# Cross-attention queries of a two-layer encoder by seven half-width products instead of eight

## The chip, the cores and the metric

The program runs on one core of one Trainium2 chip, in one launch. Its time is the device time in microseconds (us), the median of several executions. Beside the times there is one execution taken by the hardware profiler; all durations below come from it.

The engines are named as in the profile: PE is the matrix engine (PEld its weight loads), DVE the vector engine, ACT the scalar engine, POOL the general-purpose engine, SP the engine that only issues transfers.

## The reference, cut to what matters

The model has two layers over 512 positions of width 1024. Each layer is a mixer, a cross-attention to a memory of 256 rows, and a gated feed-forward block with a short convolution. The change touches the cross-attention, and what stands just ahead of it:

```python
x = x + mixed                                        # mixed = mixer's heads @ w_out
x = x + memory_cross_attention(rms_norm(x, xattn_norm[layer]), rms_norm(mem, mem_norm[layer]),
                               xattn_wq[layer], xattn_wkv[layer], xattn_wo[layer])

def memory_cross_attention(xn, memn, wq, wkv, wo):   # 4 heads of 256
    q = split_heads(xn @ wq, 4)                      # 512x1024 @ 1024x1024
    k, v = split(memn @ wkv, 2)
    logits = einsum('bhqd,bhmd->bhqm', q, k) * 256 ** -0.5
    p = softmax(logits, axis=-1)
    return merge_heads(einsum('bhqm,bhmd->bhqd', p, v)) @ wo
```

`rms_norm(x, gain)` is `x * rsqrt(mean(x*x) + eps) * gain`: one factor for each position (the inverse root) and one for each channel (the gain). All of it is float32.

## The kernel before, in words

**Numbers in two parts.** A float32 operand is split into a rounded part (`hi`, a copy by ACT) and the rest (`lo`, a subtraction by DVE). A product of two operands is then three matmuls (`mm3`, lines 291 to 293). A weight block is 128 x 1024: loaded by SP into `raw` (three buffers), copied by ACT into `wh` (L285), subtracted by DVE into `wl` (L282).

**Layout.** Channels lie on partitions: x is eight tiles `x[k]` of 128 channels x 512 positions, and `xh[k]`, `xl[k]` are the two parts of x times the gain, without the inverse root. A block of the projection is 8 channel blocks x 3 = 24 matmuls of 128 x 512, all into one PSUM bank.

**Mixer's output projection** (`p_out`). For each m of 8, 24 matmuls make output block m; DVE adds it into `x[m]` (`xadd`, L619), then `xprep` makes `xh[m]`, `xl[m]` (ACT L603, DVE L604) and adds the squares of x (ACT L597, DVE L598).

**Cross-attention** (`xattn`). `x_norm` sums the squares over channels by two matmuls (L497), takes the inverse root in eight steps of DVE and ACT, and leaves it spread over all partitions in `rb`. For each head h of 4: two key blocks (two heads' worth were already made during the mixer by `p_fill`), two query blocks of 24 matmuls each, whose evacuation multiplies by `rb` and splits (`query`: DVE L1177, ACT L285, DVE L282), the value blocks for every second head, four score tiles of 6 matmuls each with their softmax (maximum L1213, exponential L1214, reciprocal L1218), the transposes, and the weighted values. Then the output projection, again by `p_out`, which also makes four `forms` of x for the feed-forward block.

**The feed-forward block already uses seven products.** 21 of its 22 pairs of blocks are done by a scheme of Strassen and Winograd (`seven` in `ffn_steps`): a 2 x 2 block product by seven products of half size, with sums of weight quarters (`sa`, made by a load and a second load that POOL issues and that adds in memory, L1505; `sb`, by DVE) and sums of x quarters (`form_steps`, L1280 to L1296). Each of its products is 12 matmuls of 128 x 256.

**Order.** The kernel's own planner (`Plan`) takes items by priority as their inputs and buffers become ready and writes the instructions of all engines in one fixed order; each engine then runs its own list strictly in that order, waiting on semaphores. The feed-forward block has a second planner (`Sched`). Both orders are decided when the program is built.

Of the kernel before, what the change touches and what calls it, by code (L numbers as in the profile page):

```python
# [236 lines left out]
class Builder:  # L237
# [475 lines left out]
    def q_parts(self, ps):  # L713
        nc, mp = self.nc, self.mp
        tq = self.til(mp, "tmp")
        nc.vector.scalar_tensor_tensor(out=tq[:], in0=ps[:], scalar=-0.125, in1=self.rb, op0=ALU.mult, op1=ALU.mult)
        out = []
        for s in range(2):
            a, b = slice(64 * s, 64 * s + 64), slice(64 - 64 * s, 128 - 64 * s)
            qa = self.til(mp, f"qa{s}", dtype=F32R, bufs=2)  # L720
            nc.scalar.copy(qa[a, :], tq[a, :])
            self.sub(qa[b, :], tq[a, :], qa[a, :])
            out.append(qa)
        return out

    def k_parts(self, ps, par):
# [4 lines left out]
        for s in range(2):  # L731
            a, b = slice(64 * s, 64 * s + 64), slice(64 - 64 * s, 128 - 64 * s)
            ka = self.til(mp, f"ka{s}", dtype=F32R, bufs=2)
# [110 lines left out]
    def mix0(self):  # L844
        nc, t, tc = self.nc, self.t, self.tc
        with tc.tile_pool(name="mix0", bufs=1, reuse_waits="tile") as mp:
            self.mp = mp
# [9 lines left out]
            mh, ml = ([None if k in (2, 3) else mp.tile([P, SEQ], F32R, name=f"{n}{k}") for k in range(8)] for n in ("mh", "ml"))  # L857
# [123 lines left out]
            for p_ in range(4):  # L981
# [41 lines left out]
                def weigh(p_=p_, pts=[i[2] for i in items], v=v):  # L1023
# [10 lines left out]
                    if mh[p_] is None:  # L1034
                        mh[p_], ml[p_] = (self.til(mp, ("ka", "qa")[p_ - 2] + i, dtype=F32R) for i in "01")
# [11 lines left out]
            self.p_out(pl, t["wo0"], lambda: (mh, ml), kd, "xat", 0, [4, 5, 6, 7, 0, 1, 2, 3], 100, True, self.memnorm)  # L1047
            pl.run()
# [73 lines left out]

    def xattn(self, layer):
        nc, t, tc = self.nc, self.t, self.tc
        with tc.tile_pool(name=f"xa{layer}", bufs=1, reuse_waits="tile") as mp:
            self.mp = mp
            pl = Plan(self.plan, [st["banks"][0] for st in self.fills], s=2, w=2, e=4, q=2, pt=2, wt=3)
            for tag, n, bufs in (("sa", 1024, 3), ("ra", 512, 1)):
                self.til(self.kp, tag, (P, n), bufs=bufs)
            kv = [self.til(self.kp, f"kv{i}", (P, 1024), F32R, bufs=1) for i in range(8)]  # L1130
            self.pad(self.kp, 128)
            kth, ktl = ([v[:].rearrange("p (a b) -> p a b", b=MEM) for v in vs] for vs in (kv[:2], kv[2:4]))
            vh, vl = kv[4:6], kv[6:]
            for tag in ("tmp", "nh"):
                self.til(mp, tag, bufs=1 + (tag == "tmp"))
            self.pad(mp, 64)
            for tag in ("qh0", "ql0", "qh1", "ql1"):
                self.til(mp, tag, dtype=F32R)
            self.pad(mp, 192)
            for tag in ("pth", "ptl"):  # L1140
                self.til(mp, tag, (P, 2, 512), F32R)
            norm = self.x_norm(pl, (mp, "nh", 1), 0, deps=self.xdone[7])
            mh, ml = [None] * 8, [None] * 8
            kd = {}
            ve = []
            for h in range(4):
                p = 10 + 10 * h
                ke = []
                for m in (2 * h, 2 * h + 1):

                    def keys(ps, m=m, at=0):
                        tmp = self.til(mp, "tmp")
                        nc.vector.tensor_tensor(out=tmp[:, :MEM], in0=ps[:, at : at + MEM], in1=self.memrb, op=ALU.mult)
                        self.split(kth[m // 4][:, m % 4, :], ktl[m // 4][:, m % 4, :], tmp[:, :MEM])

                    kc = (("D", 0.34), ("A", 0.34), ("D", 0.34))
                    if m < 2 * len(self.fills):
# [3 lines left out]
                                lambda keys=keys, st=st, m=m: keys(st["ps"], at=m % 2 * MEM), 0, (), p, free=("acc",) if m % 2 else (), chain=kc, st=st,  # L1161
# [6 lines left out]
                            pl, t["xk"][layer, m], self.mems, keys, kc, prio=p, n=MEM, per=4, off=OFF  # L1168
                        )
                    )  # L1170
                qs = {}
                qe = []
                for d in range(2):

                    def query(ps, d=d, qs=qs):
                        tmp = self.til(mp, "tmp")
                        nc.vector.scalar_tensor_tensor(out=tmp[:], in0=ps[:], scalar=0.0625, in1=self.rb, op0=ALU.mult, op1=ALU.mult)  # L1177
                        qs[d] = (self.til(mp, f"qh{d}", dtype=F32R), self.til(mp, f"ql{d}", dtype=F32R))
                        self.split(qs[d][0][:], qs[d][1][:], tmp[:])

                    qe.append(
                        self.p_proj(
                            pl, t["xq"][layer, 2 * h + d], self.xs, query, (("D", 0.66), ("A", 0.52), ("D", 0.6)), kdeps=self.xdone, edeps=[norm], prio=p, eorder=list(qe),
                            etake=("q",) if d == 0 else (),
                        )
                    )
                if h % 2 == 0:
# [5 lines left out]
                    ve = self.p_proj_tok(pl, t["xv"][layer, h // 2], self.mems, 2, values, prio=p)  # L1193
                pts = {}

                def ptget(pts=pts):
                    pts["h"] = self.til(mp, "pth", (P, 2, 512), F32R)
                    pts["l"] = self.til(mp, "ptl", (P, 2, 512), F32R)

                got = pl.add(ptget, 0, qe, p + 5, take=("pt",))  # L1200
                ss, ts = [], []
                for i in range(4):
# [3 lines left out]
                    def score(h=h, qs=qs, res=res, sl=sl):  # L1206
                        sp = self.bank("s")
                        for d in range(2):
                            kb = 2 * h + d
                            self.mm3(sp[:, :MEM], qs[d][0][:, sl], qs[d][1][:, sl], kth[kb // 4][:, kb % 4, :], ktl[kb // 4][:, kb % 4, :], d == 0, d == 1)  # L1210
# [3 lines left out]
                        nc.scalar.activation(e[:], sp[:, :MEM], AF.Exp, bias=sm[:, 0:1], accum_out=sm[:, 1:2])  # L1214
# [12 lines left out]
                    a = pl.add(score, 3 * MM, ke + qe, p + 5, take=("s", "e"), free=("s",), chain=(("D", 0.35), ("A", 0.5)))  # L1227
# [5 lines left out]
                for d in range(2):  # L1233

                    def weigh(h=h, d=d, pts=pts):
# [5 lines left out]
                        mh[b], ml[b] = (self.til(mp, "mixed", dtype=F32R, bufs=8) if h < 2 else self.til(self.memp, "mem", dtype=F32R, bufs=8) for _ in range(2))  # L1241
                        self.split(mh[b][:], ml[b][:], ps[:])

                    ws.append(pl.add(weigh, 6 * MM, ts + ve, p + 5, take=("w",), free=("w",), chain=(("A", 0.5), ("D", 0.6))))
# [3 lines left out]
            self.forms = []  # L1248
            used = [d for k in kd for d in kd[k]]

            def form(k):
                th, tl = (self.til(self.kp, f"kv{i + k}", (P, 1024), F32R, bufs=1) for i in (0, 4))
# [3 lines left out]
                f, r = self.til(mp, "pth", (P, 2, 512)), self.til(mp, "ptl", (P, 1024))  # L1256
                for fn in self.form_steps(k, layer, f, r, th, tl):
                    fn[1]()

            for k in range(4):  # L1260
                pl.add(
                    lambda k=k: form(k), 0, [*used, *self.xdone[2 * k + 1]], 100 + 2 * k + 2, order=[last_form] if k else [],
                    chain=(("A", 1.5), ("D", 1.4), ("A", 1.0), ("D", 1.2)) if k < 3 else (),
                )
                last_form = pl.items[-1]
# [3 lines left out]
    def form_steps(self, k, layer, t, r, th, tl):  # L1269
# [6 lines left out]
            t[:, j, :], self.x[2 * k + j][:], AF.Identity, scale=self.col("ffn", layer * 8 + 2 * k + j)  # L1276
# [16 lines left out]
    def ffn_steps(self, layer, mp):  # L1293
# [22 lines left out]
        RAWS = {"raw": (self.wp, 1024, 3), "dr": (mp, 512, 2), "sa": (self.kp, 1024, 3), "sb": (mp, 512, 2), "ra": (self.kp, 512, 1)}  # L1316
# [81 lines left out]
        small_ = lambda tag: [self.til(mp, tag + i, dtype=F32R, bufs=1) for i in "hl"]  # L1398
        act_ = lambda: tuple(self.til(mp, i, dtype=F32R, bufs=10) for i in ("ah", "al"))
        self.pad(mp, 64)  # L1400
        for tag in ("s2", "a22", "s4"):
# [662 lines left out]
```

## Time and profile before

| what | value |
|---|---|
| median of 3 executions | 1464.67 us (1464.3 to 1464.98) |
| the profiled execution: its time, its span | 1464.19 us, 1462.4 us |
| PE busy | 1447.1 us, 99% of the span |
| weight loads (PEld) busy | 1272.8 us, 87% |
| DVE busy | 1219.0 us, 83% |
| ACT busy | 891.0 us, 61% |
| TensorE clock granted over the span | 0.999 |
| layer 0: mixer's output projection; queries, keys, values and attention; its output projection | about 217 to 262; 262 to 345; 345 to 408 us |
| layer 1: the same | about 923 to 968; 968 to 1051; 1051 to 1115 us |

A busy PE is a PE with matmuls in flight: they overlap, so a matmul's duration (0.39 us for 128 x 512) is longer than the step from its start to the next one's. The price of a matmul is that step. Instructions of DVE and ACT overlap their neighbours a little too, so there also the step from start to start counts where they stand in a row.

### The profile page before, as it was taken

The numbers are of one execution on the slowest core, as the hardware profiler recorded it, in microseconds if no ns is written. First come the engines' busy times: TensorE is split into PE (matmuls) and PEld (weight loads), VectorE is DVE, ScalarE is ACT, GpSimd is POOL, SyncE is SP. The second block draws the span as 40 slices with busy tenths as digits, with TensorE's granted clock in tenths as the row PEclk, the third lists the DMA queues.
The fourth block names the chain that finished last, engine by engine and source line by source line (L and its number), as shares of the span: only waits on it lengthen the run. The fifth ranks groups of instructions, "written<-read, shape, count | busy, mean of one in ns | idle before, by whom it ended". The sixth has DMA issues, their size and how long they took to land.

```text
span 1462.4 us, 23179 instructions
## 1 busy us (share of the span) xinstructions
PE 1447.1 (99%) x8719; PEld 1272.8 (87%) x8719; DVE 1219.0 (83%) x2172; ACT 891.0 (61%) x1581; POOL 67.9 (5%) x108
## 2 busy tenths in 40 slices
PE   9999999999999999999999999999999999999998
PEld 7888787888899999999888888888888999999987
DVE  7789985766799999999769988676569999999974
ACT  7688664544577666666447665455456766656654
POOL 0001120000000000000000100000000000000000
PEclk9999999999999999999999999999999999999999
DMA  5222433723246666662223332363323666665322
GB/s 199 87 74 73 122 117 123 209 87 116 87 133 164 170 170 159 155 163 75 84 101 109 115 102 68 128 175 121 115 83 112 157 182 168 158 164 153 110 69 76
DMA packets 67297, 183.91 MB, mean 126 GB/s; under 512 B 7264, under 2 KB 7264, under 8 KB 67184
## 3 DMA queue, kind: packets, MB, share of 16 engines
q1 hardware_dynamic: 60128, 159.28, 34.0%
q0 software_dynamic: 6048, 22.02, 8.7%
q8 instruction: 68, 1.11, 0.3%
q10 hardware_dynamic: 1008, 1.12, 0.2%
q14 instruction: 45, 0.37, 0.1%
HBM read 180.27 MB, written 2.13 MB: 125 GB/s over the span
## 4 chain that ended last, share of the span: by engine, by line
PE 82%; DVE 11%; ACT 3%; issue 2%; DMA 1%; POOL 0%; SPq 0%; DVEq 0%; ACTq 0%; POOLq 0%
PE acc L291 16%; PE acc L292 16%; PE acc L293 16%; PE w L292 5%; PE w L293 5%; PE w L291 5%; PE s L293 3%; PE s L291 3%; PE s L292 3%; DVE wl L282 2%; PE acc L352 2%; PE acc L354 2%; PE acc L353 2%; DVE c L1449 1%; PE w L800 1%
## 5 line engine op out<-in xcount | busy, mean ns | idle before, releaser
L291 PE MATMUL acc<-xh,wh 128*128 128x512 f32 (+1 forms) x752 | 258.0, 343 | 0.1
L293 PE MATMUL acc<-xh,wl 128*128 128x512 f32 (+1 forms) x752 | 255.9, 340 | 0.2 <-DVE wl L282 0.2
L292 PE MATMUL acc<-xl,wh 128*128 128x512 f32 (+1 forms) x752 | 255.6, 340 | 0.0
L282 DVE TENSOR_TENSOR wl<-raw,wh 128x1024 fp32r<-128x1024 f32 (+2 forms) x193 | 228.9, 1186 | 23.3 <-ACT wh L285 22.7
L285 ACT CAST wh<-raw 128x1024 fp32r<-128x1024 f32 (+1 forms) x135 | 139.2, 1035 | 139.1 <-PE acc L292 85.5
L293 PEld LDWEIGHTS acc<-xh,wl 128*128 128x128 f32 x752 | 141.2, 188 | 17.3 <-DVE wl L282 0.6
L291 PEld LDWEIGHTS acc<-xh,wh 128*128 128x128 f32 x752 | 141.4, 188 | 16.6 <-ACT v L1685 0.6
L292 PEld LDWEIGHTS acc<-xl,wh 128*128 128x128 f32 x752 | 141.3, 188 | 16.1
L1449 DVE SCALAR_TENSOR_TENSOR c<-hs,vec,c 128x512 f32<-128x512 f32 x176 | 128.0, 744 | 6.9 <-ACT c L1442 5.9
L293 PE MATMUL w<-ah,wl 128*128 128x512 f32 x304 | 119.0, 392 | 0.0
L292 PE MATMUL w<-al,wh 128*128 128x512 f32 x304 | 118.6, 390 | 0.0
L291 PE MATMUL w<-ah,wh 128*128 128x512 f32 x304 | 118.5, 390 | 0.0
L1442 ACT ACTIVATE c<-hs,vec 128x512 f32<-128x512 f32 x88 | 70.8, 815 | 35.9 <-DVE hs L1589 35.3
L293 PEld LDWEIGHTS w<-ah,wl 128*128 128x128 f32 x304 | 57.1, 188 | 12.1
L619 DVE TENSOR_TENSOR x<-w,x 128x512 f32<-128x512 f32 x72 | 49.4, 686 | 20.0 <-PE w L293 20.0
L291 PEld LDWEIGHTS w<-ah,wh 128*128 128x128 f32 x304 | 57.1, 188 | 9.9
L292 PEld LDWEIGHTS w<-al,wh 128*128 128x128 f32 x304 | 57.1, 188 | 9.9
L1505 POOL DMA_DIRECT2D sa<-in_up_dram x42 | 36.1, 860 | 610.2 <-DMA sa<-in_up_dram 162.1
L1520 ACT CAST wh<-sa 128x1024 fp32r<-128x1024 f32 x42 | 44.1, 1050 | 32.5 <-PE w L292 24.0
L291 PE MATMUL acc<-mem,wh 128*128 128x256 f32 (+1 forms) x192 | 61.1, 318 | 0.0
L292 PE MATMUL acc<-mem,wh 128*128 128x256 f32 (+1 forms) x192 | 60.9, 317 | 0.0
L293 PE MATMUL acc<-mem,wl 128*128 128x256 f32 (+1 forms) x192 | 60.7, 316 | 0.0
(475 smaller groups left out, 4190.9 us busy)
## 6 DMA issues: line engine op xcount, KB each, us to landing
raw<-in_up_dram SPq DMA_DIRECT2D x46, 512.0 KB, 3.5
sa<-in_up_dram SPq DMA_DIRECT2D x42, 512.0 KB, 3.9
sa<-in_up_dram POOLq DMA_DIRECT2D x42, 512.0 KB, 5.8
dr<-in_down_dram SPq DMA_DIRECT2D x64, 256.0 KB, 3.1
ra<-in_up_dram SPq DMA_DIRECT2D x42, 256.0 KB, 2.6
raw<-in_xk_dram SPq DMA_DIRECT2D x16, 512.0 KB, 4.3
raw<-in_wo_dram SPq DMA_DIRECT2D x16, 512.0 KB, 3.6
raw<-in_xq_dram SPq DMA_DIRECT2D x16, 512.0 KB, 3.3
```

What stands on the lines that cost most here:

```text
L282: self.nc.vector.tensor_tensor(out=lo, in0=v, in1=hi.bitcast(F32), op=ALU.subtract)
L285: self.nc.scalar.copy(hi, v)
L291: mm(out, wh, xh, start=first, stop=False, skip_group_check=parts)
L292: mm(out, wh, xl, start=False, stop=False, skip_group_check=parts)
L293: mm(out, wl, xh, start=False, stop=last, skip_group_check=parts)
L352: mm(ps, xh[k][:, ts], wh[:, ws], start=(k == 0), stop=False)
L353: mm(ps, xh[k][:, ts], wl[:, ws], start=False, stop=False)
L619: self.nc.vector.tensor_tensor(out=self.x[m][:], in0=ps[:], in1=self.x[m][:], op=ALU.add)
L1442: nc.scalar.activation(st["c_"][:, j, :], hs()[:, j, 2:514], AF.Identity, scale=self.col("cw", (layer * 3 + 2) * 44 + blk), bias=self.col( ...
L1449: nc.vector.scalar_tensor_tensor(out=c, in0=hs()[:, j, n : n + 512], scalar=w, in1=c, op0=ALU.mult, op1=ALU.add)
L1505: return add("POOL", 0.0029 * cols, lambda: nc.gpsimd.dma_start(out(), src(), accum_op=ALU.add), deps, due, (), (), 6.0)
L1520: nc.scalar.copy(s["wh"][:, :cols], raw())
```

## The change

The query projection of each head is computed by the feed-forward block's scheme: the head's two blocks of 128 query channels and the two halves of 256 positions make a 2 x 2 block product over the halves (even and odd blocks) of the input channels, done by seven products of 12 matmuls of 128 x 256.

- `p_forms`, called at the end of both mixers' plans, closes the mixer's tile pool, opens the pool that the cross-attention and the feed-forward block share, issues the first loads of weight sums, makes the forms of x for the block pairs 0 to 2 during the output projection, and issues the first product of heads 0 and 1.
- `p_query` is one head's seven products. Heads 0 and 1 are interleaved in finer pieces around the arrival of the last block of x (`x[7]`); heads 2 and 3 follow whole.
- The fourth form is made at the start of `xattn` (`last`).
- The evacuation no longer multiplies by the inverse root. `x_norm` goes; four matmuls of 128 x 2 (`rsqrt_cols`) and twelve DVE instructions of four columns make the inverse root for 128 positions per partition, and the exponential takes it as its scale. The maximum is multiplied by it first, one DVE instruction of one column for each score tile.
- Keys that were made during the mixer, all other keys, and the values are evacuated only after all four heads' products, because the forms lie in the tiles where keys and values will lie (`opened`, priority 45; heads now have priority 50 and up).
- Tiles that outlive the mixers move to pools of their own (`out0`, `out1`); several tiles of `xattn` and of the feed-forward block share buffers under new names.

```diff
+    def p_forms(self, pl, layer, mix, used):
+        def opened():
+            mix.close()
+            self.kp = self.keys.enter_context(self.tc.tile_pool(name=f"keys{layer}", bufs=1, side="right", reuse_waits="tile"))
...
+            for h in range(3):
+                self.sum_load(layer, h)
+        def form(k):
...
+            for fn in self.form_steps(k, "xat", layer, f[:, :1024].rearrange("p (a b) -> p a b", a=2), r[:, :1024], th, tl):
+                fn[1]()
+        last = pl.add(opened, 0, used, 100, order=[self.memnorm])
+        for k in range(3):
+            last = pl.add(
+                lambda k=k: form(k), 0, self.xdone[2 * k + 1], 100 + 2 * k + 2, order=[last], chain=(("A", 1.5), ("D", 1.4), ("A", 1.0), ("D", 1.2))
+            )
...
+    def sum_load(self, layer, h):
+        sa = self.sums[h] = self.til(self.kp, "sa", (P, 1024), bufs=3)
+        a1, a2 = self.t["xq"][layer, 2 * h], self.t["xq"][layer, 2 * h + 1]
+        pair = self.t["xq"][layer].rearrange("(h j) p c -> h p j c", j=2)[h]
+        self.nc.sync.dma_start(sa[:].rearrange("p (a b) -> p a b", a=2), pair[:, :, :512])
+        self.nc.gpsimd.dma_start(sa[:], a2, accum_op=ALU.add)
...
+    def p_query(self, pl, layer, h, order):
...
+        def product(w, c, xs, bank, first, ks=range(4)):
+            for k in ks:
+                at = slice(c + k * P, c + (k + 1) * P)
+                self.mm3(st[bank][:, :256], w[0][:, at], w[1][:, at], *xs(k), first and k == 0, k == 3, True)
...
+        def p1():
+            st["raw"] = self.til(self.wp, "raw", (P, 1024), bufs=3)
+            nc.sync.dma_start(st["raw"][:], a1)
...
+            st["f3"] = self.parts(OFF)
+            self.split(*st["f3"], st["raw"][:])
+            st["X"] = self.bank("w")
+            product(st["f3"], 0, X(0, 0), "X", True)
+        def seed():
+            st["Y"] = self.acc_bank(st["banks"][0])
+            nc.scalar.activation(st["Y"][:, :256], st["X"][:, :256], AF.Copy, scale=-1.0)
+        def p5():
+            st["f1"] = self.parts(OFF)
+            self.split(*st["f1"], self.sums[h][:])
+            st["R"] = self.bank("s")
+            product(st["f1"], 512, T1, "R", True, range(4 - (h == 0)))
+        def kept(n, bank):
+            st[n] = self.til(mp, "xe", (P, MEM), bufs=4)
+            nc.scalar.copy(st[n][:], st[bank][:, :256])
+        def p6():
+            st["sb"] = self.til(self.kp, "sb", bufs=2)
+            tt_(out=st["sb"][:], in0=self.sums[h][:, 512:], in1=st["raw"][:, :512], op=ALU.add)
...
+            wide("s2", st["sb"][:])
+            product(st["s2"], 0, T2, "Y", False, range(4 - (h == 0)))
+        def c11():
+            st["hs"] = self.til(mp, "hs", (P, 1088))
+            nc.scalar.copy(quarter(0, 0), st["X"][:, :256])
+        def p3():
+            tt_(out=st["sb"][:], in0=st["sb"][:], in1=st["raw"][:, 512:], op=ALU.add)
+            wide("s4", st["sb"][:])
+            product(st["s4"], 0, X(1, 1), "R", False)
+        def p4():
+            wide("a22", self.rest[:])
...
+            product(st["a22"], 0, T4, "Y", False)
...
-            norm = self.x_norm(pl, (mp, "nh", 1), 0, deps=self.xdone[7])
+            norm = pl.add(
+                lambda state=self.state: rs.append(self.rsqrt_cols(state["sq"], SEQ, 256.0 / DM, 256.0 * EPS)), 0.4, self.xdone[7], 2.5, take=("s",), free=("s",), chain=(("D", 2.3),)
+            )
...
-                    def query(ps, d=d, qs=qs):
-                        tmp = self.til(mp, "tmp")
-                        nc.vector.scalar_tensor_tensor(out=tmp[:], in0=ps[:], scalar=0.0625, in1=self.rb, op0=ALU.mult, op1=ALU.mult)
-                        qs[d] = (self.til(mp, f"qh{d}", dtype=F32R), self.til(mp, f"ql{d}", dtype=F32R))
-                        self.split(qs[d][0][:], qs[d][1][:], tmp[:])
...
-                        nc.scalar.activation(e[:], sp[:, :MEM], AF.Exp, bias=sm[:, 0:1], accum_out=sm[:, 1:2])
+                        r = rs[0][:, i : i + 1]
+                        nc.vector.tensor_tensor(out=sm[:, 3:4], in0=sm[:, 0:1], in1=r, op=ALU.mult)
+                        nc.scalar.activation(e[:], sp[:, :MEM], AF.Exp, scale=r, bias=sm[:, 3:4], accum_out=sm[:, 1:2])
...
-    a["xq"] = np.stack([col_blocks(i["xattn_wq"][n]) for n in range(2)])
+    a["xq"] = np.stack([even_odd(col_blocks(i["xattn_wq"][n])) for n in range(2)])
```

251 lines of the change are left out of this document (186 added, 65 removed).

## The prediction

> **What bounds the kernel now.** I read the engines' shares first, then the chain that ended last, then the stretches that the change touches.
>
> ```profile
> span 1462.4 us, 23179 instructions
> PE 1447.1 (99%) x8719; PEld 1272.8 (87%) x8719; DVE 1219.0 (83%) x2172; ACT 891.0 (61%) x1581; POOL 67.9 (5%) x108
> ...
> PE 82%; DVE 11%; ACT 3%; issue 2%; DMA 1%; POOL 0%; SPq 0%; DVEq 0%; ACTq 0%; POOLq 0%
> ```
>
> PE is busy 99% of the span and carries 82% of the chain. The next view is the windows of all engines over layer 0's cross-attention: the mixer's output projection, the inverse root with the first queries, the rest up to the attention's output projection.
>
> ```profile
> core 0: us, PE busy (x) PEld busy (x) DVE busy (x) ACT busy (x) POOL busy (x), PEclk, DMA share, GB/s
> 217.00:262.00 45.00, 44.01 (x203) 34.99 (x202) 26.25 (x39) 18.98 (x29) 0.00 (x0) 1.00 0.40 128
> 262.00:283.00 21.00, 21.00 (x94) 17.35 (x93) 16.72 (x26) 12.34 (x20) 2.74 (x3) 1.00 0.96 270
> 283.00:345.00 62.00, 62.00 (x367) 54.78 (x366) 41.22 (x83) 31.20 (x64) 0.00 (x0) 1.00 0.34 113
> ```
>
> From 262 to 345 PE never stops, at full clock, so a matmul removed there is time removed, as long as the other engines keep up. DVE has 84.19 of 128 us taken, ACT 62.52: 43.8 and 65.5 us are free.
>
> **The change part by part.** *The matmuls.* The windows of PE show a stretch of 128x512 steps and one of the feed-forward block's 128x256 products; the timeline of PE shows twelve steps of each kind.
>
> ```profile
> core 0: us, PE busy (x), PEclk, DMA share, GB/s
> 240.00:260.00 20.00, 20.00 (x90) 1.00 0.29 97
> 425.00:445.00 20.00, 19.81 (x169) 1.00 0.55 147
> ```
>
> ```profile
> 261.66 0.39 PE L291 MATMUL acc<-xh,wh 128*128 128x512 f32 x1
> ...
> 264.38 0.39 PE L291 MATMUL acc<-xh,wh 128*128 128x512 f32 x1
> ...
> 267.79 0.39 PE L497 MATMUL s<-rb,ones 128*128 128x512 f32 x1
> ```
>
> ```profile
> 424.48 0.28 PE L291 MATMUL s<-xh,s4h 128*128 128x256 f32 x1
> ...
> 425.84 0.28 PE L291 MATMUL acc<-kv,wh 128*128 128x256 f32 x1
> ```
>
> A wide step is 2.72/12 = 0.2267 us, a narrow one 1.36/12 = 0.1133, exactly half. Per layer 8 blocks x 24 = 192 wide ones go (43.52) and 4 heads x 7 x 12 = 336 narrow ones come (38.08): 5.44 less. `x_norm`'s two wide matmuls (0.45) give way to four of 128x2, which cost between nothing and a narrow step each (0 to 0.45): even. The order on PE outside the two cross-attentions is unchanged.
>
> *What PE waits for between products.* In 425 to 445 the 169 matmuls take 20.00 us with 0.19 without work, where 169 x 0.1133 = 19.15 is the bare price. The surplus, 0.85 over some 14 products, is 0.06 each and partly wider instructions in that window. I take 0.03 for each of the 28 products of a layer, 0.84; the bounds are 0 (as in 262 to 345, no idle time) and 0.06 (1.7).
>
> *DVE and ACT.* Their steps, start to start, from their timelines (half a row's x2 where two are grouped):
>
> ```profile
> 255.74 0.69 DVE L619 TENSOR_TENSOR x<-acc,x 128x512 f32<-128x512 f32 x1 [2.09 <-PE acc L293]
> 256.60 1.22 DVE L282 TENSOR_TENSOR wl<-raw,wh 128x1024 fp32r<-128x1024 f32 x1 [0.17 <-ACT wh L285]
> 257.74 0.74 DVE L604 SCALAR_TENSOR_TENSOR xl<-x,vec,xh 128x512 fp32r<-128x512 f32 x1
> 258.40 0.68 DVE L598 TENSOR_TENSOR sq<-sq,sqt 128x512 f32<-128x512 f32 x1
> 261.18 0.69 DVE L619 TENSOR_TENSOR x<-acc,x 128x512 f32<-128x512 f32 x1 [2.09 <-PE acc L293]
> 261.79 0.74 DVE L1153 TENSOR_TENSOR tmp<-acc,memrb 128x256 f32<-128x256 f32 x2
> 262.45 1.21 DVE L282 TENSOR_TENSOR wl<-raw,wh 128x1024 fp32r<-128x1024 f32 x1
> ```
>
> ```profile
> 260.95 1.05 ACT L285 CAST wh<-raw 128x1024 fp32r<-128x1024 f32 x1 [3.24 <-PE acc L292]
> 261.91 0.72 ACT L603 ACTIVATE xh<-x,vec 128x512 fp32r<-128x512 f32 x1
> 262.54 0.62 ACT L597 ACTIVATE sqt<-x 128x512 f32<-128x512 f32 x1
> 263.06 0.70 ACT L285 CAST kv<-tmp 128x256 fp32r<-128x256 f32 x2
> ```
>
> DVE: 1024 columns 1.14, 512 columns 0.61 (`xl` 0.66), 256 columns 0.33. ACT: 0.96, 0.52 (with a gain 0.63), 0.35. Per layer DVE loses eight `wl` (9.1), sixteen wide steps of the queries' evacuations (9.8) and `x_norm`'s six (3.7): 22.6. It gains for each head three of 1024, five of 512, two of 256 (7.13, x4 = 28.5), for each form one of 1024, one of 512, two of 256 (2.41, x4 = 9.6), and 28 tiny ones:
>
> ```profile
> L1218 DVE RECIPROCAL sm<-sm x32: 137/163/166, 286.7 to 1072.4; 128x1 f32<-128x1 f32 x32
> ```
>
> at most 0.16 each, 0 to 4.5. Net +16 to +20 us, inside the 43.8 free. ACT loses 8 x (0.96 + 0.52) = 11.8 and gains 4 x (3 x 0.96 + 3 x 0.52 + 4 x 0.35) = 23.4 and 4 x (2 x 0.63 + 0.96) = 8.9: +20, inside 65.5. So over the stage both are hidden; what counts is where the work crowds.
>
> *The end of the mixer's output projection.* A block of it lasts 261.18 - 255.74 = 5.44, and DVE rests 2.09 of it. Between x[6]'s and x[7]'s addition the new list of DVE is: x[6] 0.61, the form's rest 1.14, head 1's `wl` 1.14, `xl` 0.66, squares 0.61, the rests of `s4` and `a22` and head 2's `sb` 3 x 0.61: 6.0. That is more than the 5.44 of the block, so x[7]'s addition is 0.55 late. Behind it stand `wl` of head 0's second operand 1.14, `xl` 0.66, squares 0.61, the last form's 0.61 + 2 x 0.33 and two keys' evacuations 2 x 0.33, then ACT's copy of the form 1.05 (its full duration, since DVE waits for its end) and DVE's rest of it 1.22. From x[7] on that makes 0.55 + 0.61 + 1.14 + 0.66 + 0.61 + 0.61 + 1.32 + 1.05 + 1.22 = 7.8, some 8.2 with the hand-overs of 0.17 in the rows. In that time PE has, without needing the last form: head 0's and 1's first products 2.72, three quarters of their second ones 2.04, of head 0's fifth and sixth 2.04, the last quarters 0.68, the four tiny ones up to 0.45: 7.5 to 7.9. So x[7] and the last form just about meet PE, with 0.3 open either way: I take none.
>
> *A buffer freed late.* Head 0's `R` (L1217's copy to `xe`) must be read by ACT before PE may write its third product into the same bank. ACT comes to it behind a weight copy 0.96, two of 256 columns 0.70 and the copy itself 0.36, from about 8.0 after x[7]'s block: free at 10.0. PE arrives at 9.05 (7.48 as above, about 0.2 for tiny ones, the seventh product's 1.36). The copy's duration is that of the same-sized one in the feed-forward block:
>
> ```profile
> L1559 ACT ACTIVATE acc<-acc x42: 357/368/378, 420.9 to 1396.6; 128x256 f32<-128x256 f32 x42
> ```
>
> I charge 0.95 a layer; bounds 0 and 1.9 (if head 1 waits likewise).
>
> *Loads.* Each head's `sa` is one load by SP and one that POOL issues and that adds in memory. Page rows and the source row of the same pair in the feed-forward block, and SP's timeline row of the loads of x ahead of them:
>
> ```profile
> sa<-in_up_dram SPq DMA_DIRECT2D x42, 512.0 KB, 3.9
> sa<-in_up_dram POOLq DMA_DIRECT2D x42, 512.0 KB, 5.8
> ...
> raw<-in_xq_dram SPq DMA_DIRECT2D x16, 512.0 KB, 3.3
> ```
>
> ```profile
> 213.50 9.22 SPq L618 DMA_DIRECT2D x<-in_x_dram  x8
> ```
>
> ```profile
> 239.42 0.69 DVE L619 TENSOR_TENSOR x<-acc,x 128x512 f32<-128x512 f32 x1 [2.09 <-PE acc L293]
> ```
>
> Head 0's `sa` is issued on SP behind the x loads at 213.50 + 9.22 = 222.7 and is whole at 222.7 + 3.9 + 5.8 = 232.4; its first reader, DVE's sum for `s2`, stands behind x[3]'s addition, 239.42 + 0.61 = 240.0: 7.6 to spare. Head 0's `raw` waits for a buffer until the `wl` of block 5, about 236.2, and lands at 239.5: 0.5 to spare, and about 4.5 more until PE would feel it, because DVE is idle 2.09 a block. POOL has no other issue there (none busy in 217 to 262), and the loads of `wo` behind `sa` on SP come blocks before they are used. Cost 0. If that cover goes, the delay passes to x[4]'s addition.
>
> *The exponential.* Scale by a pointer instead of a constant is the step from a plain to a gained activation above, about 0.1 on ACT, and one tiny DVE instruction ahead of it. PE does at least 2.7 us of other products between a score and its transpose: 0. Dropping `rb` from the evacuation takes the inverse root off the queries' path; it was not on PE's path either (no idle time from 262): 0.
>
> *The sum.* Per layer 5.44 - 0.84 - 0.95 = 3.65; two layers 7.3. The profiled execution took 1464.19 us (span 1462.4 and 1.8 around it), 0.48 under the median. 1464.67 - 7.3 = 1457.4 for the median.
>
> **The rivals.** *A: all waits hidden.* Then 10.9 less: 1453.8. For it speaks PE's unbroken 62.00 of 62.00; against it the 0.19 in the products' own stretch.
>
> *B: DVE falls behind and stays behind.* If its instructions don't overlap (durations 1.22, 0.74, 0.69 in place of 1.14, 0.66, 0.61), the list before x[7] is 0.6 longer and the chain behind it 0.5; further lags of the same kind at the ends of the fourth products, where DVE's subtraction (L1193) lets PE into the bank, make some 3.5 to 4 a layer in place of 1.8: 1.6 a layer is left, 1461.4 (1459.5 to 1463.5). For it: DVE was busy 16.72 of 21 just there and gets most of the new work; against it: from 283 on it has a third of its time free.
>
> *C: slower, by a load read late in DVE's fixed list.* DVE now waits for `raw` and `sa` ahead of x[4]'s, x[5]'s and x[7]'s additions. Everything behind waits, the additions and so PE too. It costs its lateness beyond 0.5 + 4.5, and decides when it exceeds those by 3.65: a landing of 3.3 + 8.7 = 12 us. The DMA share of 0.40 there and the x loads' 1.2 us apiece speak against it; the share of 0.96 in the next window for it. A landing of 16 us would be late by 12.7, cost 7.7 and leave the layer 4.05 slower than before: 1472.8.
>
> *D: slower, because weight loads set the step.* A narrow product loads as many weights per half the columns.
>
> ```profile
> L291 PEld LDWEIGHTS acc<-xh,wh 128*128 128x128 f32 x752 | 141.4, 188 | 16.6 <-ACT v L1685 0.6
> ```
>
> The gain is gone when a narrow step costs 43.52/336 = 0.1295. At a load's 0.188 it would be 336 x 0.188 - 43.52 = 19.6 a layer more, 1504. The timeline's 0.1133 with the same loads speaks against it: loads overlap.
> The Trainium skill, "TensorE: Matmul & The Clock Gate", section "Back-to-back issue gap", says that the spacing of load and matmul pairs doesn't fall in proportion to the columns: about 81 ns at 128 and 131 at 512. A line between them is an estimate of 98 at 256, three quarters of the wide one, by which this change would cost 336 x 0.098 - 192 x 0.131 = +7.8 us a layer; this case's rows, where the narrow step is half the wide one, do not agree.
>
> *E: the change doesn't do what it says.* The instruction orders have exactly 336 narrow matmuls more and 194 wide ones fewer in each layer: excluded.
>
> **How the numbers follow.** Main case 0.68 (its own range 1455.0 to 1459.7, from waits of 0.6 to 3 a layer), A 0.08, B 0.16, C 0.05, D 0.03. 0.2%, about what can be told from no change, is 2.9 us: faster means under 1461.7. A and the main case are faster, B two thirds (0.10, its middle is below that bound): a little is taken off for costs I see nowhere, 0.82. Same: the rest of B and a little of the main case, 0.09. Slower: C, D and an unseen wait, 0.09. The range leaves out D, C and B's upper end, and reaches to A: 1453.8 to 1462.3.
>
> **What would show it.** Right: PE's count up by 286 or so, the narrow steps at 0.1133 in the query products, DVE and ACT up by about 37 and 40 us over the span, PE still without idle time in the attention, one wait of about 1 us for `xe` (L1217) a layer. Wrong: idle PE time ended by DVE `x` (L619), by `kv` (L282) or by `hs` (L1193) of more than 1 us a layer; a DVE wait for `raw` or `sa` at L1221; narrow steps over 0.12 within a product.

## The result and the profile after

The changed kernel is slower: 1472.82 us (median of 5, 1469.39 to 1474.4) against 1464.3 (1463.9 to 1464.98), a ratio of 1.0054 with a 95% interval of 1.0039 to 1.0069. Its times also spread more than those of before. The forecast was 1457.4, in a range of 1453.8 to 1462.3.

The page of the changed kernel: span, the engines' shares, and the chain that ended last.

```profile
span 1471.8 us, 24027 instructions
...
PE 1445.4 (98%) x9019; PEld 1281.5 (87%) x9019; DVE 1258.1 (85%) x2284; ACT 931.1 (63%) x1655; POOL 75.1 (5%) x116
...
PE 75%; DVE 14%; ACT 5%; issue 3%; DMA 3%; POOL 0%; SPq 0%; DVEq 0%; ACTq 0%; POOLq 0%
```

PE is busy 1.7 us less than before and the span is 9.4 us longer, so the time in which PE does nothing grew from 15.3 us (1462.4 - 1447.1) to 26.4 (1471.8 - 1445.4): more than what was gained in matmuls was lost as waiting. DVE is up by 39.1 us and ACT by 40.1, as forecast (37 and 40). DMA has come into the chain with 3%, from 1.

Where the time went is read from the timeline of DVE, from the starts of the additions into x[0] and x[7] in each output projection (us, layer 0 / layer 1; the profiled execution of each kernel):

| stretch | before | changed | difference |
|---|---|---|---|
| mixer's output projection, x[0] to x[7] | 33.72 / 33.74 | 39.83 / 35.60 | +6.11 / +1.86 |
| cross-attention, from there to its own x[7] | 146.69 / 146.77 | 146.75 / 147.53 | +0.06 / +0.76 |
| feed-forward block, to its last addition | 336.80 / 304.21 | 336.99 / 304.48 | +0.19 / +0.27 |

These differences make 9.25 of the 9.4 us. 7.97 lie in the mixers' output projections, where the forecast had x[7]'s addition 0.55 late in each layer, and the cross-attentions show no gain where 3.65 a layer was forecast.

The waits of PE in the changed kernel, layer 0 and layer 1 (columns: engine, tile and line that waited, what ended the wait, us in total, times, longest):

```profile
engine line waited for: us in total, times, longest us
PE acc L291 <- ACT acc L1207: 2.5, 1, 2.5
PE w L291 <- ACT acc L1207: 2.1, 1, 2.1
PE acc L291 <- DVE x L619: 2.0, 2, 1.7
PE w L292 <- DVE xl L604: 0.7, 1, 0.7
```

```profile
PE acc L291 <- ACT acc L1207: 2.1, 1, 2.1
PE w L291 <- ACT acc L1207: 0.8, 1, 0.8
```

L1207 is `seed`, the copy by which ACT starts a head's second accumulation (0.36 us). It is the last link each time, but it is not slow: it stands behind something in ACT's list. The timeline of ACT at both places of layer 0 tells what:

```profile
268.33 0.72 ACT L603 ACTIVATE xh<-x,vec 128x512 fp32r<-128x512 f32 x1 [1.41 <-DVE x L619]
268.96 0.36 ACT L1207 ACTIVATE acc<-w 128x256 f32<-128x256 f32 x1
...
292.64 0.62 ACT L285 CAST a<-ra 128x512 fp32r<-128x512 f32 x1 [2.81 <-DMA ra<-in_xq_dram]
293.17 0.37 ACT L1207 ACTIVATE acc<-w 128x256 f32<-128x256 f32 x1
```

At 268.96 head 0's copy had stood behind the cast of x[7], which waited for DVE's addition; at 293.17 head 2's had stood behind a cast of the last weight quarter (`ra`), which waited for its load. Why DVE added x[7] so late is in its own timeline:

```profile
239.75 0.69 DVE L619 TENSOR_TENSOR x<-acc,x 128x512 f32<-128x512 f32 x1 [0.86 <-PE acc L293]
246.32 0.69 DVE L1221 TENSOR_TENSOR sb<-sa,raw 128x512 f32<-128x512 f32 x1 [5.88 <-DMA raw<-in_xq_dram]
...
261.06 0.68 DVE L619 TENSOR_TENSOR x<-acc,x 128x512 f32<-128x512 f32 x1
...
267.61 0.69 DVE L619 TENSOR_TENSOR x<-acc,x 128x512 f32<-128x512 f32 x1
```

Behind x[3]'s addition the sum of head 0's weight quarters waited 5.88 us for `raw`, and everything behind it waited too. In layer 1 the same instruction waited 1.6. The timeline of SP has this `raw` issued at 236.51 (the row merges four loads and gives the first one's start), and the source view of that line has 9.7 us as the longest time from issue to landing, which is this load's:

```profile
236.51 22.20 SPq L1197 DMA_DIRECT2D raw<-in_xq_dram  x4
...
DMA to landing us min/median/max: 3.0/3.3/9.7
```

The forecast took 3.3 us from the page, and the kernel before's own load at this place (issued at 236.09) landed after 3.2. The windows of all engines show what it met, first of the kernel before, then of the changed one:

```profile
222.00:231.00 9.00, 8.01 (x38) 5.11 (x37) 4.60 (x8) 4.84 (x8) 0.00 (x0) 1.00 0.29 90
231.00:246.00 15.00, 15.00 (x67) 12.41 (x67) 9.37 (x13) 6.27 (x9) 0.00 (x0) 1.00 0.41 138
```

```profile
222.00:231.00 9.00, 8.00 (x39) 5.06 (x37) 4.49 (x8) 4.58 (x8) 1.86 (x2) 1.00 0.87 269
231.00:246.00 15.00, 15.00 (x68) 12.43 (x67) 8.55 (x12) 8.64 (x13) 0.85 (x1) 1.00 0.87 225
246.00:262.00 16.00, 14.29 (x64) 11.52 (x63) 15.36 (x23) 8.00 (x11) 0.00 (x0) 1.00 0.29 99
```

The last two columns are the DMA engines' share and GB/s: from 222 to 246 they are 0.87 busy where they were 0.29 and 0.41. Of the sums' loads for three heads, SP's halves had landed by 231.3; POOL's adding halves landed at 237.3, 241.8 and 245.0, so all three were still under way when `raw` was issued. And once `raw` is there, DVE is busy 15.36 of 16 us up to 262: it has no room in which to catch up.

### The profile page after: what moved, and what is told of

It reads as the page before. It is cut to its first block, busy times and chain, and to the rows that moved or that the text cites. A ratio compares the mean times of both kernels' runs of the same rounds, so it can differ in the third digit from the quotient of the medians.

```text
span 1471.8 us, 24027 instructions
## 1 busy us (share of the span) xinstructions
PE 1445.4 (98%) x9019; PEld 1281.5 (87%) x9019; DVE 1258.1 (85%) x2284; ACT 931.1 (63%) x1655; POOL 75.1 (5%) x116
## 4 chain that ended last, share of the span: by engine, by line
PE 75%; DVE 14%; ACT 5%; issue 3%; DMA 3%; POOL 0%; SPq 0%; DVEq 0%; ACTq 0%; POOLq 0%
PE acc L291 13%; PE acc L292 13%; PE acc L293 13%; PE w L293 6%; PE w L291 6%; PE w L292 6%; PE s L293 3%; PE s L291 3%; PE s L292 3%; DVE wl L282 3%; PE acc L352 2%; PE acc L354 2%; PE acc L353 2%; DVE c L1656 1%; DMA raw<-in_xq_dram 1%
## 5 line engine op out<-in xcount | busy, mean ns | idle before, releaser
L282 DVE TENSOR_TENSOR wl<-raw,wh 128x1024 fp32r<-128x1024 f32 (+3 forms) x185 | 218.8, 1183 | 30.8 <-ACT wh L285 27.6
L291 PE MATMUL acc<-xh,wh 128*128 128x256 f32 (+1 forms) x624 | 206.9, 332 | 0.1
L293 PE MATMUL acc<-xh,wl 128*128 128x256 f32 (+1 forms) x624 | 205.8, 330 | 0.2 <-DVE wl L282 0.2
L292 PE MATMUL acc<-xl,wh 128*128 128x256 f32 (+1 forms) x624 | 205.6, 329 | 0.0
L291 PEld LDWEIGHTS acc<-xh,wh 128*128 128x128 f32 x624 | 117.2, 188 | 12.1 <-ACT v L1893 0.6
L292 PEld LDWEIGHTS acc<-xl,wh 128*128 128x128 f32 x624 | 117.2, 188 | 11.5
L282 DVE TENSOR_TENSOR s<-sb,s 128x512 fp32r<-128x512 f32 x100 | 68.6, 686 | 5.5 <-ACT s L285 5.5
L293 PEld LDWEIGHTS w<-ah,wl 128*128 128x128 f32 x304 | 57.1, 188 | 11.9
L282 DVE TENSOR_TENSOR wl<-sa,wh 128x1024 fp32r<-128x1024 f32 x50 | 61.1, 1221 | 5.6 <-ACT wh L1727 3.2
L1727 ACT CAST wh<-sa 128x1024 fp32r<-128x1024 f32 x42 | 44.1, 1049 | 34.3 <-PE w L292 26.4
L619 DVE TENSOR_TENSOR x<-w,x 128x512 f32<-128x512 f32 x72 | 49.5, 688 | 18.1 <-PE w L293 18.0
L1545 ACT CAST wh<-dr 128x512 fp32r<-128x512 f32 x64 | 39.6, 618 | 39.2 <-issue 35.5
L1727 ACT CAST s<-sb 128x512 fp32r<-128x512 f32 x84 | 52.1, 620 | 18.5 <-PE s L293 14.6
```

Of the source, the lines that this page charges most:

```text
L282: self.nc.vector.tensor_tensor(out=lo, in0=v, in1=hi.bitcast(F32), op=ALU.subtract)
L291: mm(out, wh, xh, start=first, stop=False, skip_group_check=parts)
L292: mm(out, wh, xl, start=False, stop=False, skip_group_check=parts)
L293: mm(out, wl, xh, start=False, stop=last, skip_group_check=parts)
L619: self.nc.vector.tensor_tensor(out=self.x[m][:], in0=ps[:], in1=self.x[m][:], op=ALU.add)
L1545: nc.scalar.copy(st["wh"][:, :cols], st[tag][:, :cols])
```

## The experiments

Theory T: three loads and additions hold in-order lists of DVE and ACT, and PE's loss is theirs. R: DVE simply has too much to do around x[7]. S: the place of ACT's copies is the price. None of the kernels leaves out any of the computation. Each group ran beside the kernel before on one chip. `behind(a, b)` only orders a after b in the list of their engine.

### Three orders, one at a time

**DVE's sum behind x[5]'s addition.**

```diff
+            if h == 0:
+                self.behind(total, self.mark["add", 5])   # total: the sum at L1221
```

> Edit: on DVE the sum of head 0's weight quarters (L1221, which waits for raw) is issued behind x[5]'s addition instead of ahead of x[4]'s; all work is the same. Theory T (three waits at the head of in-order lists cost the time: raw on DVE, x[7] and ra on ACT): the 5.9 us wait of layer 0 and the 1.6 us wait of layer 1 on DVE disappear, x[7]'s addition comes up to 6 us earlier in layer 0, and PE loses about 4 us less in layer 0 and up to 1 us less in layer 1: 1467 to 1469 us, with less spread from run to run. Rival R (the added 39 us of DVE work are too much around x[7], whatever its order): x[7]'s addition stays late by the work ahead of it, 1471 to 1473.

Measured: 1467.23 us, ratio 1.0021 (1.0012 to 1.0030). The waits for `raw` are gone, and the mixer's stretch is 33.72 and 33.76 us, as in the kernel before, with all of DVE's new work still in it. R would have had it late. In layer 1 nothing was won, though: the mixer's stretch is 1.84 us shorter than in the changed kernel and the cross-attention 1.76 longer (149.29 against 147.53), with a wait of PE of 2.5 us for head 2's copy. This order moved some matmuls of head 0's third and head 1's fifth products on PE as well; the run isn't clean in that.

**ACT's copy of head 0 ahead of x[7].**

```diff
+            if gain == "xat" and k == 7:
+                self.behind(self.mark["xh"], self.mark["seed", 0])
```

(and the squares of x[7] and the gained part of the last form behind head 0's copy likewise; head 1's copy is put behind that part and ahead of the squares)

> Edit: on ACT the copies of heads 0 and 1 that start the second accumulation (L1207) are issued ahead of the work that waits for x[7]; all work is the same. Rival S (the place of these copies on ACT is itself the price): the waits of 2.28 and 0.27 us in layer 0 and 1.00 and 0.27 in layer 1 go, 3.8 us less, 1469. Theory T: x[7] stays as late as before, so PE meets the next thing made from it, the last form (kv, L282), and loses nearly the same there: 1472 to 1473 (at most 1 us less).

Measured: 1468.08, ratio 1.0026 (1.0015 to 1.0037). That is less than T said, but the intervals of this ratio and of the control below (1.0024 to 1.0049) overlap. The edit does only half of what was announced: head 0's copy now runs before x[7]'s cast, but head 1's stays behind it, and PE waits 1.4 us there. Layer 0 took 186.4 us from the mixer's x[0] to the attention's x[7] (changed kernel 186.6, control 185.6): the wait moved. These three numbers can't be held against each other more closely than some 1.6 us, because in this run and in the control the clock was halved once in layer 0 (last section). The run doesn't settle S alone.

**ACT's cast of `ra` behind the copy, heads 2 and 3.**

```diff
-            wide("a22", self.rest[:])
+            a22 = wide("a22", self.rest[:])
+            if h > 1:
+                self.behind(a22[0], st["seed"])
```

> Edit: on ACT the copy of head 2's and head 3's last weight quarter (a22, from ra, L285) is issued behind the same head's copy that starts the second accumulation (L1207), so that a late load of ra no longer holds that copy; all work is the same. Theory T: the waits of 2.70 us in layer 0 and 2.25 in layer 1 go, 4 to 5 us less: 1468 to 1469. Rival R (DVE and ACT have too much to do): the wait only moves to the next product, 1471 to 1473.

Measured: 1466.98, ratio 1.0019 (1.0010 to 1.0028), although `raw` was late here too (4.8 us). In layer 0 PE's waits for L1207 fell to the one behind x[7]:

```profile
PE w L296 <- ACT acc L1212: 2.1, 1, 2.1
PE acc L296 <- DVE x L624: 1.0, 2, 0.7
PE w L297 <- DVE xl L609: 0.7, 1, 0.7
```

(Lines shift a little from kernel to kernel: L1212 is the same copy here, L624 the addition into x, L609 the rest of the gained x.) The 2.5 us have not moved on: T.

### The orders together

The three orders, and `behind` for three instructions of DVE (the rests of `s4` and `a22` of head 0, the sum of head 2), after the last form's subtractions.

> Edit: the three orders together, and on DVE three instructions that nothing needs soon (the rests of s4 and a22 of head 0, the sum of head 2) behind the last form's subtractions instead of ahead of x[7]'s addition; all work is the same. Theory T: of the some 17 us that PE loses beyond the kernel before in the two cross-attentions about 13 go: 1458 to 1462, faster than the kernel before. Rival R: the DVE work remains, x[7] and the last form stay late, 1468 to 1472.

Measured: 1460.44, ratio 0.9976 (0.9966 to 0.9986): faster than the kernel before, with the same matmuls and the same work on DVE and ACT as the changed kernel. R is out.

### The control, and which orders matter

> The changed kernel once more, beside the next three on one chip, so that each order's gain can be read against it: 1469 to 1474 us if the first measurement holds for this chip; nearer to 1468 if the three single orders before looked better than they are by the chip they ran on.

The changed kernel once more: 1469.91 (1468.5 to 1472.16), ratio 1.0037 (1.0024 to 1.0049). It is slower on this chip also, by 5.5 us where the first group had 8.5; `raw` was waited for 4.5 us here instead of 5.9. The gains of the single orders above, which ran on another chip, are therefore nearer to 2 to 3 us each than to the 5 to 6 that the first median suggests.

Two orders, the sum's and the cast's:

> Edit: only two of the orders: DVE's sum of head 0 behind x[5]'s addition, and ACT's copy of a22 for heads 2 and 3 behind the copy that starts the second accumulation. Theory T (raw and ra held two in-order lists; the rest is little): the two single gains add, 1461 to 1463 us, within 2 us of all orders together. Rival S (where ACT has the copies of heads 0 and 1 behind x[7] costs 3 us by itself): 1464 to 1466.

Measured: 1462.47, ratio 0.9983 (0.9975 to 0.9992), 7.4 below the control. Within T's 1461 to 1463. The two single gains, 2.7 and 2.9 against this control, add up to less than 7.4; the profiles of both single runs have a stretch of halved clock (last section) and this run's has none, which would be worth 1.6 us more, but no run shows that by itself.

### The crowd of loads

```diff
-            for h in range(3):
-                self.sum_load(layer, h)
+            self.sum_load(layer, 0)
...
+                for i in (1, 2):
+                    self.behind(self.sum_load(layer, i), first)   # first: head 0's raw
```

> Edit: the loads of the weight sums of heads 1 and 2 are issued on SP behind head 0's raw instead of some 13 us ahead of it; the lists of PE, DVE and ACT are those of the changed kernel. Theory T (raw is late because the sums' loads of three heads fill the DMA engines ahead of it): raw lands within 4 to 5 us of its issue, DVE's wait for raw falls under 1 us, and the time is that of the run with the later sum, 1466 to 1469; if the sums of head 1 then come late, up to 2 us of it is lost again. Rival Q (raw is late because its buffer comes free late or because of its place on SP's queue): no change against the changed kernel.

Measured: 1464.84, ratio 1.0002 (0.9993 to 1.0011), 5.1 below the control and faster than T's 1466 to 1469. This is the cleanest run: PE, DVE, ACT and POOL have the changed kernel's lists, one for one. `raw` was issued at 235.91, and its reader, at 239.77, didn't wait: it landed in under 3.9 us. The timeline of DVE, to be held against the 5.88 above (L624 is L619, L1228 is L1221):

```profile
239.16 0.69 DVE L624 TENSOR_TENSOR x<-acc,x 128x512 f32<-128x512 f32 x1 [0.88 <-PE acc L298]
239.77 0.68 DVE L1228 TENSOR_TENSOR sb<-sa,raw 128x512 f32<-128x512 f32 x1
```

The mixer's stretch is 34.27 us in layer 0 and 34.25 in layer 1: 0.55 and 0.51 more than before. Q is out: `raw` left at nearly the same time as before (235.91 and 236.51), so neither its buffer nor its place on SP's list had held it; what changed is what else was on its way, above all POOL's adding loads for heads 1 and 2. Whether those weigh more than plain loads of the same size was not tried. This also agrees with the Trainium skill, "DMA: Bandwidth & Descriptors", section "Issuing engines are not separate DMA queues": transfers run on the same 16 engines whichever engine issued them, so that POOL's adding loads and SP's plain ones share them.

What is left in layer 0 is the other load, `ra` (L1214 is the copy L1207):

```profile
PE acc L296 <- ACT acc L1214: 2.4, 1, 2.4
PE acc L296 <- ACT qa L286: 0.7, 1, 0.7
PE acc L296 <- DVE x L624: 0.3, 1, 0.3
PE s L296 <- ACT xe L1224: 0.3, 1, 0.3
```

### A small copy moved

All orders, and ACT's copy of the fifth product (L1217) ahead of two copies into `hs`.

> Edit: all the orders of the fourth run, and on ACT the copy of head 0's fifth product (xe, L1217) ahead of the two copies into hs (L1229). The wait of 0.48 us a layer before head 0's third product goes: 1459.3 to 1460 us if nothing else is late there, 1460.4 as before if it moves to the next product; about 1459 is what is left when PE's other waits stay as they are.

Measured: 1460.34, ratio 0.9973 (0.9962 to 0.9984). No change: the 0.48 us went, and a little later PE waits for DVE's subtraction (`hs`, L1193 in the changed kernel) instead, 0.34 us in layer 0 and 0.59 in layer 1.

### A second buffer for `ra`

> Edit: a second buffer for ra (the last weight quarter), so that the load for the next head needn't wait until DVE is done with this head's; on ACT and DVE one copy and its rest stand one place earlier for head 2, all else is the same. Theory T (ACT's copy that starts head 2's second accumulation is held by the late ra ahead of it): ACT no longer waits for ra, PE's wait of 1.9 to 2.7 us a layer before head 2's product goes, 4 us less than the changed kernel on the same chip, as with the later copy. Rival S (the copies' place among ACT's casts is late anyway): under 1.5 us less.

Measured: 1473.63, ratio 1.0070 (1.0057 to 1.0083), which none had expected. By stretches it comes apart. ACT waits for `ra` in neither layer, and the cross-attention is 144.25 and 145.46 us (changed kernel 146.75 and 147.53): T held there. But the second `ra` load went out in the crowd (11.9 us to land), `raw` was as late as ever (10.0 us; the mixer's stretch 40.09 where it was 39.83), and both feed-forward blocks, of which the edit changes little but the place of tiles, took 339.94 and 307.25 us instead of 336.99 and 304.48.

### The two load remedies, and all remedies

> Edit: the two load remedies alone: sums of heads 1 and 2 issued behind head 0's raw, and ACT's copy of a22 (heads 2 and 3) behind the copy that starts the second accumulation. PE's and nearly all of DVE's lists are those of the changed kernel. Theory T: with raw and ra off the path the seed copies wait no more, though they still stand behind x[7]'s cast: 1460 to 1461.5 us, as with all orders. Rival S: 1462 to 1464.

Measured: 1460.73, ratio 0.9975 (0.9966 to 0.9984). With `raw` and `ra` off the path the copies may stay behind x[7]'s cast: PE waits 0.29 us for one in layer 0. S is out as a cause of its own: these two remedies, and no move of a copy ahead of x[7], bring nearly all that any run won.

> Edit: the later loads of sums, the later copy of a22, ACT's copies of heads 0 and 1 ahead of x[7]'s cast, and the three DVE instructions behind the last form: all remedies but the moved sum. Nothing is left that waits for a load: 1459.5 to 1461 us. Below 1459.5 would say that the moved sum of the fourth run cost something itself.

Measured: 1459.81 (1459.2 to 1462.56), ratio 0.9972 (0.9963 to 0.9981): the lowest median of all, 4.6 us below the kernel before; the runs with 1460.34, 1460.44 and 1460.73 can't be told from it. Page and PE's waits in layer 0 (L1229 is the copy L1217, L629 the addition into x):

```profile
span 1457.4 us, 24022 instructions
...
PE 1442.1 (99%) x9019; PEld 1280.3 (88%) x9019; DVE 1258.7 (86%) x2284; ACT 930.9 (64%) x1655; POOL 74.1 (5%) x116
```

```profile
PE acc L296 <- ACT qa L286: 0.7, 1, 0.7
PE s L296 <- ACT xe L1229: 0.3, 1, 0.3
PE acc L296 <- DVE x L629: 0.3, 1, 0.3
```

DVE's and ACT's busy time is the changed kernel's within 0.6 us. Two of the three waits are the kernel before's; the wait for `xe` is new.

### The padding

The second buffer above had to take 128 bytes of padding at the end of the pool that the feed-forward block shares. The kernel of all remedies without that padding:

```diff
-            self.pad(self.kp, 128)
+            self.pad(self.kp, 0)
```

> Edit: the kernel of the four remedies without the 128 bytes of padding (per partition) at the end of the pool that the cross-attention and the feed-forward block share. The second buffer for ra had to take that room, and both feed-forward blocks were some 3 us longer in that run. If the place of the tiles in memory makes the feed-forward block's matmuls slower, both blocks are longer here too, 337.0 to about 340 and 304.4 to about 307 us, and the run takes 1465 to 1466 us. If it was the second buffer itself (its loads), nothing changes: 1459.5 to 1461.

Measured: 1466.44, ratio 1.0013 (1.0004 to 1.0022), 6.6 above the same kernel with the padding on another chip, and a little above the 1465 to 1466 that was expected. All engines' lists are the same, one for one. The feed-forward blocks took 339.88 and 307.25 us against 336.96 and 304.45, and the cross-attentions were 1.1 and 0.5 us longer as well. The second buffer's run has the same feed-forward blocks within 0.06 us, so it too lost this much to the place of its tiles; without it, as an estimate, it would have come to about 1467, 3 below the control.

## Why the prediction was wrong

**The matmuls: right, a little too good.** I take the length from the start of the last matmul of the mixer's output projection to that of the attention's, and as bare time the number of matmuls times the median step of their width over the whole run (0.227, 0.114, 0.109 and 0.112 us for 512, 256, 128 and 2 columns); what the length has beyond it counts as waits. Worked out from all PE rows, good to some tenths (layer 0 / layer 1):

| | length | waits | bare |
|---|---|---|---|
| before | 146.70 / 146.76 | 1.01 / 1.08 | 145.69 / 145.68 |
| changed | 150.50 / 149.01 | 9.65 / 8.17 | 140.85 / 140.84 |
| all remedies | 143.82 / 143.69 | 2.96 / 2.84 | 140.86 / 140.85 |

The bare time falls by 4.84 a layer; the forecast was 5.44. D, with weight loads as the bound, is out: the narrow step is 0.114 and not 0.1295 or more. Of the 0.6 missing, some 0.4 is the tiny matmuls of the inverse root: they were said to be even with `x_norm`'s 0.45, but there are eight of them on PE, and they take 0.81 (timeline of PE in the run with all orders, from their first start to the next product's) to 0.90 (eight steps):

```profile
268.09 0.95 PE L457 MATMUL s<-ones,sq 128*128 128x2 f32 x8
268.90 0.36 PE L296 MATMUL w<-xh,wh 128*128 128x256 f32 x1
```

The rest, 0.16, is the rounding of the steps: with 0.227 and 0.114 the exchange of 192 wide for 336 narrow matmuls is worth 5.28.

Not all of the changed kernel's 8.17 in layer 1 is waiting: 1.6 us of it are matmuls at half the clock (last section).

**The waits between products and the late buffer: right in size.** 0.84 + 0.95 = 1.79 a layer was charged; with the loads out of the way the waits are 1.95 and 1.76 above before's. The named one, `xe` (L1217) before the third product, is there in both layers, 0.48 instead of 0.95.

**The end of the mixer's output projection: right where no load is late.** x[7]'s addition was to be 0.55 late by DVE's list; in the run with later sums it is 0.55 and 0.51.

**The loads: wrong, and this is the step that failed.** "Cost 0" rested on 3.3 us for head 0's `raw` and 0.5 + 4.5 us to spare. Two things were wrong in it. The 3.3 was the page's median of the kernel before, whose load at this place met DMA engines that were 0.41 busy; the change itself sends three heads' sums ahead of it, 1 MB each in two loads, and the landing took 9.7 us at a share of 0.87. The share of 0.40 that was held against rival C was that of the kernel before, without these loads. And the 4.5 us of patience weren't there: DVE's rest of 2.09 a block, on which they were counted, is used up by the forms' work of the same part of the prediction. Only C's mechanism was right, at 0.05; it was to decide from a landing of 12 us, and with DVE full it decided earlier. That C's own example, a landing of 16 us, comes to 1472.8 us as measured is chance: `raw` took 9.7, and `ra`, which C doesn't have, took its share. DVE did fall behind and stay behind, as B had it, but a load put it there and not the length of its own instructions.

**What no step had.** `ra` has one buffer and is read by ACT ahead of head 2's copy: its load could go out only when DVE had finished with head 1's (286.25 on SP), met the feed-forward block's first loads, and took 6.4 us. The working followed the queues of SP, POOL and DVE, and asked of ACT's list only what stood before one copy. Which instruction stands behind a load there decides 2.5 and 2.1 us of PE. The Trainium skill, "PSUM — Partial Sum Buffer", section "Engine vs sequencer instructions", has the rule: the queues of ACT, DVE and POOL are strictly first in, first out. The timeline of ACT above agrees: head 2's copy ran at 293.17, behind the cast of `ra` at 292.64.

Added up, in profiled spans: forecast -7.3; the bare time 1.2 short; waits beyond the charged ones 6.9 and 5.3 inside the cross-attentions (8.64 and 7.09 above before's, less 1.79 each; 1.6 of the 5.3 is the halved clock), 2.0 in layer 0's mixer stretch; the feed-forward blocks 0.5. That makes +8.6 of the +9.4.

**The sign.** 0.82 on faster was too much. Two of the signs that were named for being wrong are there: idle PE time ended by DVE `x` (L619), 2.0 us in layer 0, and DVE's wait for `raw` at L1221. The gain was real, and the kernel with all remedies has 4.6 us of the 7.3; but its margin of 3.65 a layer was to be spent by two waits on loads, and both were priced from a profile in which those loads don't exist.

## What to carry to other kernels

A load's landing time is a property of its stretch: where a change adds transfers, count their bytes into the windows of the new kernel before the old median is used, and give a load that something urgent waits for the first place. For each added instruction that waits for a load, look up what stands behind it in its engine's fixed list and who waits for that; a copy of 0.36 us cost PE 2.5. If a change's work is hidden by rests of an engine, those rests can't also be the slack for lateness.

## What the runs showed of the hardware

**After a wait of PE of 2 us or more its clock was halved for 3.41 us, in some cases.** Windows of PE in layer 1 of the changed kernel, around the wait of 2.1 us that ended at 1001.41 (the third number from the end is the granted clock):

```profile
995.00:1002.60 7.60, 5.51 (x48) 1.00 0.74 213
1002.70:1006.00 3.30, 3.30 (x18) 0.50 0.49 134
1006.10:1012.00 5.90, 5.90 (x54) 1.00 0.69 228
```

From 1002.86 to 1006.20 a narrow matmul steps 0.213 us in place of 0.114, which costs 1.6 us. Of the 14 profiled executions of this case, six have such a stretch before their last 20 us, one of them two; each lasts 3.41 us and begins 0.2 to 1.6 us after the end of a PE wait of 2.0 to 2.8 us. The other eight have none. Not every such wait is followed by one: the waits of 2.1 and 2.5 us in layer 0 of the changed kernel were not, nor one of 2.4 us in the run with the later sums. So a long wait of PE can cost more than its length, and not the same in every execution: in the run with the later sums the two fastest executions (1462.18 and 1462.39 us) have a mean clock of 0.999 and 1.000, the three slowest (1466.21 to 1466.78) of 0.998, though those between them don't lie in that order. No run changed the length of a wait alone, so that the wait brings it about is argued and not shown.

**The 128 bytes of padding are worth some 6.6 us.** Without them the narrow matmuls themselves are slower. Windows of PE from 430 to 740 us and one group of its matmuls there (mean ns behind the comma), first with the padding, then without:

```profile
430.00:740.00 310.00, 308.79 (x2168) 1.00 0.51 141
L297 PE MATMUL acc<-kv,a 128*128 128x256 f32 x80 | 22.1, 277 | 0.0
L298 PE MATMUL acc<-kv,a 128*128 128x256 f32 x80 | 22.1, 277 | 0.0
```

```profile
430.00:740.00 310.00, 309.63 (x2160) 1.00 0.51 141
L297 PE MATMUL acc<-kv,a 128*128 128x256 f32 x80 | 22.4, 280 | 0.0
L298 PE MATMUL acc<-kv,a 128*128 128x256 f32 x80 | 22.4, 280 | 0.0
```

PE waits no more than with the padding and starts eight matmuls fewer. The median step of the 5187 narrow matmuls of a run is 0.118 us where it was 0.114, that of the wide ones 0.227 in both. The edit only shifts tiles by 128 bytes in each partition; which tile and which address do it wasn't tried.
